# Seven block products for the input projection too, its results through DRAM, the mixers as a stage of two quarters

## The chip, the cores and the metric

One core of one Trainium2 chip runs the kernel, one launch for all of the work. The metric is device time in microseconds of that core, the median of several runs: 2829.16 us before the change (three runs, 2828.21 to 2831.07).

## What is computed

A decoder trunk of one layer on 2048 positions of width 1024, in float32. With h the RMS norm of x:

```
z = h @ w_in                       # 1024 x 5632: pool 512, conv value 512, conv gate 512, u 512, v 512, three gates of 1024
y_a = pool_mixer(z_pool)           # causal means over 2, 4, 8, 16 positions, less the input, then 128 x 256 products, scaled
y_b = silu(layernorm(dwconv31(val * sigmoid(gate)))) @ conv_pw
y_c = (gelu(u) * (causal 128 x 128 mix of layernorm(gelu(v)))) @ sgu_out
x = x + (sigmoid(g0 + b) * y_a + sigmoid(g1 + b) * y_b + sigmoid(g2 + b) * y_c) @ w_out
h = rmsnorm(x); z = h @ ffn_up     # 1024 x 5632, halves g and val
x = x + (silu(dwconv3(g)) * val) @ ffn_down
out = rmsnorm(x)
```

## The kernel before

The positions are cut into four quarters of 512, and two quarters make a half. Activations lie with channels on the 128 partitions and 512 positions along the free dimension; such a tile is a "half tile" of an arena of 67 (`Arena`, L105). To keep float32 accuracy each operand is split into a rounded part `hi` (a cast on ScalarE) and the rest `lo` (a subtraction on VectorE), in `split` (L263) for activations and in `ensure` (L180, lines 192 and 193) for weights, and each 128 x 128 x 512 product is three matmuls, `mm3` (L222, lines 225 to 227).

Weights come as chunks of 128 x 1024 in the order of the list `self.seq` through SyncE's queue, two ahead; up to four are prepared (`take`, `retire`). The order of TensorE, SyncE and GpSimd is the order of the program; VectorE and ScalarE are ordered by the planner, with `high_priority` for weights.

For each half, `build` (L1001) runs `mixers` (L516) and `w_out` (L730) for its first quarter, then for its second, then `ffn_up` (L836) for both, then `down` (L907) for each quarter. `mixers` makes the 44 column tiles of w_in one by one with `next_col` (L239; eight blocks deep, 24 matmuls) or, for u and v, with `rows` (L244), uses each where it lies, and drains the conv taps (`conv_taps`, L432, 31 VectorE instructions a tile) from a queue between products. Norms, pool means (L490), sgu (L453, L516) and the conv norm (L695) stand in this one stream. `w_out` stores the new x.

`ffn_up` treats two quarters as a 2 x 2 block product (two quarters by two halves of the 1024 channels, times the two halves of the channels by two column tiles) and makes it by seven block products of four blocks each (p1 to p7, `up_order`, L78) where eight would be plain. It needs sums and differences of the activations (`first_sums`, L770, `second_sums`, L790: the blocks a11, a12, s1 to s4, a22) and of the weights (`ready_part`, L158; four subtractions of GpSimd a column pair, L161). `down` fetches the stored activations for each of its two column halves and splits them (`queue_act`, L959). The first quarter's w_in starts on raw x and applies the norm behind the product for three conv pairs (`RAW_PAIRS`).

## Time and profile before

| | |
|---|---|
| median of three runs | 2829.16 us |
| the profiled execution, its span | 2830.14 us, 2828.4 us |
| TensorE busy, instructions | 2767.2 us (98%), 11938 |
| VectorE busy | 1978.9 us (70%) |
| ScalarE busy | 1167.3 us (41%) |
| GpSimd busy | 424.9 us (15%) |
| mean granted clock of TensorE | 0.988 |
| DMA | 361.13 MB, 128 GB/s |

The profile is of one execution, so sums are made against its own 2828.4 us and the 1.7 us around it. A busy TensorE is not yet one at its best, since matmuls overlap; their pitch is read from how many fall into a stretch. PE is TensorE, DVE VectorE, ACT ScalarE, POOL GpSimd, SP SyncE; L193 is a line of the kernel.

### The profile page before, as it was taken

The numbers are of one execution on the slowest core, as the hardware profiler recorded it, in microseconds if no ns is written. First come the engines' busy times: TensorE is split into PE (matmuls) and PEld (weight loads), VectorE is DVE, ScalarE is ACT, GpSimd is POOL, SyncE is SP. The second block draws the span as 40 slices with busy tenths as digits, with TensorE's granted clock in tenths as the row PEclk, the third lists the DMA queues.
The fourth block names the chain that finished last, engine by engine and source line by source line (L and its number), as shares of the span: only waits on it lengthen the run. The fifth ranks groups of instructions, "written<-read, shape, count | busy, mean of one in ns | idle before, by whom it ended". The sixth has DMA issues, their size and how long they took to land.

```text
span 2828.4 us, 32169 instructions
## 1 busy us (share of the span) xinstructions
PE 2767.2 (98%) x11938; PEld 2231.7 (79%) x11938; DVE 1978.9 (70%) x2980; ACT 1167.3 (41%) x1628; POOL 424.9 (15%) x326
## 2 busy tenths in 40 slices
PE   8999999999899999999999999999998999999998
PEld 7888888888688887787788888888886888877886
DVE  8995889658856565555689857896688556555565
ACT  4434324253544443445434343242534444434443
POOL 1000100000332332000200301000003332330020
PEclk9999999999899999999999999999998999999999
DMA  4224332333133233566432443323332233235564
GB/s 162 90 93 153 112 127 82 104 120 127 57 115 119 90 119 108 175 216 216 171 112 82 143 167 116 120 82 97 127 119 82 90 119 111 98 112 191 204 223 156
DMA packets 130013, 361.13 MB, mean 128 GB/s; under 512 B 14624, under 2 KB 16672, under 8 KB 129856
## 3 DMA queue, kind: packets, MB, share of 16 engines
q1 hardware_dynamic: 109296, 319.60, 33.8%
q10 hardware_dynamic: 18432, 32.51, 3.0%
q0 software_dynamic: 2128, 6.96, 0.6%
q8 instruction: 93, 1.52, 0.2%
q14 instruction: 64, 0.52, 0.1%
HBM read 318.65 MB, written 40.37 MB: 127 GB/s over the span
## 4 chain that ended last, share of the span: by engine, by line
PE 92%; DVE 3%; DMA 2%; POOL 1%; ACT 1%; issue 1%; SPq 0%; DVEq 0%; POOLq 0%; ACTq 0%
PE ps L226 30%; PE ps L227 30%; PE ps L225 30%; DVE h L268 1%; DMA both<-wts 1%; DVE wlo L193 1%; POOL tw L161 1%; DMA h<-act 1%; POOL h L355 0%; DMA h<-xT 0%; ACT whi L192 0%; PE ps L603 0%; ACT h L267 0%; PE ps L305 0%; PE ps L316 0%
## 5 line engine op out<-in xcount | busy, mean ns | idle before, releaser
L225 PE MATMUL ps<-h,whi 128*128 128x512 f32 x3648 | 1442.2, 395 | 27.1 <-ACT h L267 12.1
L226 PE MATMUL ps<-h,whi 128*128 128x512 f32 x3648 | 1442.1, 395 | 19.0 <-DVE h L268 18.5
L227 PE MATMUL ps<-h,wlo 128*128 128x512 f32 x3648 | 1439.0, 394 | 2.0 <-DVE wlo L193 1.9
L225 PEld LDWEIGHTS ps<-h,whi 128*128 128x128 f32 x3648 | 689.3, 189 | 192.1 <-ACT h L267 16.3
L226 PEld LDWEIGHTS ps<-h,whi 128*128 128x128 f32 x3648 | 689.1, 189 | 191.0 <-DVE h L268 33.8
L227 PEld LDWEIGHTS ps<-h,wlo 128*128 128x128 f32 x3648 | 689.9, 189 | 160.8 <-DVE wlo L193 4.2
L192 ACT CAST whi<-raw 128x1024 fp32r<-128x1024 f32 x376 | 394.2, 1050 | 891.0 <-PE ps L226 636.2
L193 DVE TENSOR_TENSOR wlo<-raw,whi 128x1024 fp32r<-128x1024 f32 x376 | 470.2, 1252 | 340.2 <-ACT whi L192 337.7
L444 DVE SCALAR_TENSOR_TENSOR h<-cbuf,params,h 128x512 f32<-128x512 f32 x480 | 340.6, 747 | 2.5
L193 DVE TENSOR_TENSOR wlo<-tw,whi 128x1024 fp32r<-128x1024 f32 x88 | 107.8, 1225 | 309.5 <-ACT whi L192 309.3
L161 POOL TENSOR_TENSOR tw<-both 128x512 f32<-128x512 f32 x88 | 122.9, 1396 | 1239.5 <-DMA both<-wts 1064.7
L268 DVE TENSOR_TENSOR h<-h,h 128x512 fp32r<-128x512 f32 x309 | 228.0, 764 | 68.0 <-ACT h L267 64.6
L267 ACT CAST h<-h 128x512 fp32r<-128x512 f32 x309 | 189.1, 619 | 183.9 <-DMA h<-act 75.3
L192 ACT CAST whi<-tw 128x1024 fp32r<-128x1024 f32 x88 | 92.4, 1050 | 212.7 <-POOL tw L161 119.5
L161 POOL TENSOR_TENSOR tw<-both,tw 128x512 f32<-128x512 f32 x88 | 156.5, 1778 | 3.4
L992 POOL TENSOR_TENSOR h<-h,h 128x512 f32<-128x512 f32 (+1 forms) x32 | 37.4, 1178 | 423.4 <-ACT h L982 422.9
L225 PE MATMUL ps<-whi,h 128*128 128x512 f32 x256 | 101.0, 395 | 0.0
L227 PE MATMUL ps<-whi,h 128*128 128x512 f32 x256 | 100.9, 394 | 0.0
L226 PE MATMUL ps<-wlo,h 128*128 128x512 f32 x256 | 100.7, 393 | 0.0
L355 POOL TENSOR_TENSOR h<-h,h 128x512 f32<-128x512 f32 x24 | 41.1, 1749 | 392.6 <-PE ps L227 375.4
L298 ACT ACTIVATE h<-h 128x512 f32<-128x512 f32 (+1 forms) x99 | 57.4, 609 | 39.1 <-DVE h L955 12.3
L299 DVE TENSOR_TENSOR h<-h,h 128x512 f32<-128x512 f32 (+1 forms) x82 | 58.9, 718 | 12.6 <-ACT h L298 9.5
(147 smaller groups left out, 1678.6 us busy)
## 6 DMA issues: line engine op xcount, KB each, us to landing
raw<-wts SPq DMA_DIRECT2D x376, 512.0 KB, 3.6
both<-wts SPq DMA_DIRECT2D x88, 512.0 KB, 4.5
h<-act SPq DMA_DIRECT2D x176, 256.0 KB, 4.1
act<-h ACTq DMA_DIRECT2D x88, 256.0 KB, 3.0
h<-xT SPq DMA_DIRECT2D x64, 256.0 KB, 5.4
x<-h ACTq DMA_DIRECT2D x32, 256.0 KB, 4.3
h<-x SPq DMA_DIRECT2D x32, 256.0 KB, 5.0
out<-h POOLq DMA_DIRECT2D x24, 256.0 KB, 2.7
```

The costliest lines, as they stand in the source:

```text
L161: sub = lambda o, a, b: self.nc.gpsimd.tensor_tensor(o, a, b, op=ALU.subtract)
L192: nc.scalar.copy(h, src)
L193: nc.vector.tensor_tensor(l, src, h.bitcast(F32), op=ALU.subtract)
L225: mm(out, l[0], r[0], start=start, stop=False)
L226: mm(out, l[0], r[1], start=False, stop=False)
L227: mm(out, l[1], r[0], start=False, stop=stop)
L267: self.nc.scalar.copy(hi, src)
L268: self.nc.vector.tensor_tensor(lo, src, hi.bitcast(F32), op=ALU.subtract)
L298: self.nc.scalar.activation(t, x, AF.Square)
L299: eng.tensor_tensor(s, s, t, op=ALU.add)
L355: nc.gpsimd.tensor_tensor(t, x[k], rstd, op=ALU.mult)
L444: nc.vector.scalar_tensor_tensor(acc, buf[:, k:k + T], w, acc, op0=ALU.mult, op1=ALU.add)
```

## The change

w_in is made for two quarters at once by the same seven block products (`w_in` on `strassen`, which `ffn_up` now shares): 22 pairs of column tiles, in an order given by `in_pairs`. Every result goes to DRAM after its activation function (`spill`, issued on SyncE's queue by `flush` two products later) and is fetched again where it is used. The order of the seven products is another one (`up_order`). The mixers become a stage for two quarters, which holds the sgu output, conv output and w_out products and reads gates and accumulators as streams.

What lay between the products becomes jobs, generators that are stepped once or twice per product (`tick`) as long as the arena has room: the rms factors of the second half (`factors_job`), the block sums of the next seven-product stage (`rows_job`), sgu mixing (`mix_job`, now with channels transposed and four matmuls of 128 columns a row tile), the pool (`pool_job`, window sums on GpSimd) and the conv norm (`conv_job`). The conv taps are drained one or two per product. The adds of squares and of the accumulators mostly move to GpSimd, which is now ordered by the planner.

The stages run: w_in of half 0; 15 of the 22 pairs of half 1; mixers of half 0; the other 7 pairs of half 1; ffn_up of half 0; down of quarter 0; mixers of half 1; down of quarter 1; ffn_up of half 1; down of quarters 2 and 3. `down` keeps its split activations for both column halves. The norm statistics always use the narrow form, and the first stage begins on normalized x (`head_rows`). The arena has 72 tiles.

```diff
-NHALF = 67
-RAW = 2
+NHALF = 72
+RAW = 3
...
+CUT = 15
...
+def in_pairs():
+
+    conv = [("conv", i, 512 + i * P, 1024 + i * P) for i in range(4)]
+    uv = [("uv", i, 1536 + i * P, 2048 + i * P) for i in range(4)]
+    pool = [("pool", i, 2 * i * P, (2 * i + 1) * P) for i in range(2)]
+    tiles = list(range(8)) + list(range(16, 24)) + list(range(8, 16))
+    gate = [("gate", (m, n), 2560 + m * P, 2560 + n * P) for m, n in zip(tiles[::2], tiles[1::2])]
+    rest = uv + pool + gate
+    return [p for i in range(4) for p in (conv[i], rest[2 * i], rest[2 * i + 1])] + rest[8:]
...
+def up_order(first=0, end=NPAIR):
+
+
+    out = [(p, first + i) for i in range(LAG) for p in ("p1", "p2")]
+    for i in range(first, end + 1):
+        n = i + LAG - 1 if i > first else end
+        out += [("p6", i), ("p4", i - 1), ("p5", i), ("p1", n), ("p7", i), ("p2", n), ("p3", i - 1)]
+    return [(p, i) for p, i in out if first <= i < end]
...
+        self.seq = w() + w(0, CUT) + mix + w(CUT, NPAIR) + up + down + mix + down + up + down * 2
...
+            raw = []
             for h in range(2):
-                self.nc.sync.dma_start(out=raw[:, h, :], in_=self.aps["wts"][i + h * NFF])
+                raw.append(self.wpool.tile([P, 1024], F32, name="raw", tag="raw", bufs=RAW))
+                self.nc.sync.dma_start(out=raw[h], in_=self.aps["wts"][i + h * NPAIR])
...
+    def room(self):
+
+        return len(self.halves.free) - (8 * (len(BLOCKS) - len(self.S)) if self.stage == "in" else 0)
...
+    def tick(self, n=1):
+
+        for _ in range(n):
+            for jobs in self.jobs:
+                if jobs and self.room() >= self.spare + jobs[0][1]:
+                    self.step(jobs)
...
+    def spill(self, dst, keys, t, flag=None):
+
+        self.fresh.append((dst, keys, t, flag))
+
+    def flush(self, n=1):
+
+        for _ in range(n):
+            for dst, keys, t, flag in self.due:
+                self.nc.sync.dma_start(out=dst, in_=t)
+                release(keys)
+                if flag:
+                    self.there[flag] = True
+            self.due, self.fresh = self.fresh, []
...
+    def block(self, st, name, k, t):
+
+        ks, p = self.split(t)
+        if st is None:
+            self.skeys.setdefault(name, []).extend(ks)
+            self.S.setdefault(name, []).append(p)
+            return
+        for d, key, s in zip(self.blocks[st][name][k], ks, p):
+            self.spill(d, [key], s.bitcast(F32), (st, name, k))
...
+    def factors_job(self, q):
+
+        yield 3
+        s = self.half()
+        for k in range(KD):
+            keys, (t,) = self.fetch([self.aps["xT"][q, k]])
+            self.add_square(s[1], t, self.nc.gpsimd, k == 0)
+            release(keys)
+            if k % 2:
+                yield 3
+        yield from self.rstd_job(self.rstx[q], s, ("rstx", q))
...
+        for k in range(H):
+            (k0, k2), (a0, b0) = nxt
+            yield 3
+            norm(a0, k, 0)
+            norm(b0, k, 1)
+            self.block(st, "a11", k, a0)
+            ks, s3 = self.half()
+            g.tensor_tensor(s3, a0, b0, op=ALU.subtract)
+            release([k0])
+            yield 3
+            (k3,), (b1,) = self.fetch([src[q0 + 1][k + H]])
+            self.block(st, "s3", k, s3)
+            yield
+            yield 2
+            norm(b1, k + H, 1)
+            self.block(st, "a22", k, b1)
+            g.tensor_tensor(b0, b0, b1, op=ALU.add)
+            g.tensor_tensor(b1, b1, s3, op=ALU.subtract)
+            release([ks])
...
+            for k in range(4):
+                c = slice(o * T + k * P, o * T + (k + 1) * P)
+                self.mm3(ps, (w[0][:, c], w[1][:, c]), self.S[moving[p]][k], start and k == 0, k == 3, not start)
...
+            if p == "p1":
+                g["s1"] = self.half()
+                cp(g["s1"][1], ps)
+            elif p == "p2":
+                k, t = g.pop("s1")
+                tt(t, t, ps, op=ALU.add)
+                sink(i, "11", t, k)
+            elif p == "p6":
+                g["u2"] = self.half()
+                cp(g["u2"][1], ps)
+            elif p == "p7":
+                k, t = self.half()
+                cp(t, ps)
+                tt(t, t, g["c"], op=ALU.add)
+                sink(i, "22", t, k)
+            elif p == "p4":
+                sink(i, "21", ps, None)
+            elif p == "p3":
+                k, t = g.pop("u2")
+                tt(t, t, ps, op=ALU.add)
+                sink(i, "12", t, k)
+                del st[i]
+            self.flush()
+            after(n - len(order))
+        self.flush(2)
...
+        for k in range(KC):
+            go = tap(k)
+            go.first = k == 0
+            go.flags = [("ci", n, i) for n in range(max(0, q - 1), q + 1)]
+            self.bg.append(go)
...
+    def w_in(self, q0, near, late=None, part=()):
...
+        def act(dst, t, key, func, flag, **kw):
+            k, s = (key, t) if key else self.half()
+            nc.scalar.activation(s, t, func, **kw)
+            self.spill(dst, [k], s, flag)
...
+            elif kind == "uv":
+                act((self.us, self.vs)[y][q][:, m * T:(m + 1) * T], t, key, AF.Gelu_apprx_tanh, ("uv"[y], q, m))
+            elif kind == "gate":
+                act(self.gates[q][m[y]], t, key, AF.Sigmoid, ("gate", q, m[y]),
+                    bias=self.par("bgate", m[y]))
...
+            nc.gpsimd.tensor_tensor(dst[:, lo:n], src[:, lo:n], src[:, lo - m:n - m], op=ALU.add)
...
+            pm = self.bank()
+            for h in range(4):
+                hs = slice(h * P, (h + 1) * P)
+                self.mm3(pm[:, hs], (x[0][:, hs], x[1][:, hs]), (sg[0][:, hs], sg[1][:, hs]), True, True)
+            for h in range(4):
+                hs = slice(h * P, (h + 1) * P)
+                nc.vector.scalar_tensor_tensor(t[:, hs], pm[:, hs], self.par("slg", h), bt[:, hs], op0=ALU.mult, op1=ALU.add)
+            nc.vector.tensor_tensor(t, t, ut, op=ALU.mult)
+            self.spill(heads(self.gt[q])[:, :, r * P:(r + 1) * P], [key], heads(t), ("gt", q, r))
+            release(ks + [ku])
...
+                for m in range(2):
+                    ps = self.col(w, [p for _, p in src[m]], off=(j % 2) * 512, nk=4)
+                    k, s = self.gstream()
+                    if n == 0:
+                        acc[j].append(self.astream())
+                    v.tensor_tensor(s, ps, s, op=ALU.mult)
+                    ka, a = acc[j][m]
+                    (v if n and j > 5 else g).tensor_tensor(a, a, s, op=ALU.add)
+                    release([k])
+                    if n:
+                        merged[m].append(self.split(a))
+                        release([ka])
+                    elif j > 4:
+                        for _ in range(1 + (j == 7)):
+                            cT[len(cT[0]) // 4].append(self.split_next(cstream))
+                    self.flush()
+                    during(n)
...
             for k in range(n):
-                self.queue_act(q, h, k + AHEAD)
+                if h == 0:
+                    self.queue_act(q, k + 2 * AHEAD)
                 if k % 2 == 0:
                     w = self.take()
-                ks, a = self.queued.pop((q, h, k))
-                step(w, k, range(F4), slice(0, T), a)
...
-        key, t = self.half()
-        self.nc.sync.dma_start(out=t, in_=self.acts[q][k])
-        self.queued[q, h, k] = self.split(t)
+        (key,), (t,) = self.fetch([self.acts[q][k]])
+        self.queued[q, k] = self.split(t)
...
+        self.add(self.setup_sgu(), self.factors_job(2), self.factors_job(3))
+        self.add(self.rows_job("w1", 2, xT, "nmix", self.rstx[2:], [("rstx", 2), ("rstx", 3)]))
+        self.add(self.open_mix())
+        for q in (0, 1):
+            self.add(self.mix_job(q, range(NR)))
+        self.add(self.close_mix())
+        for q in (0, 1):
+            self.add(self.pool_job(q, range(4)), self.conv_job(q))
+
+
+        def near(n):
+            self.spare = 7 if n > -20 else 3
+            if n + TOTAL > 8:
+                self.tick()
+            self.drain(2 if self.there["w1"] else 1)
+            self.next_blocks("w1", n)
+
+        self.w_in(0, near, late)
...
+        self.w_in(2, near, None, (0, CUT))
...
+        self.add(self.open_mix(), side=1)
+        for r in range(NR):
+            for q in (2, 3):
+                self.add(self.mix_job(q, [r]), self.pool_job(q, [r]), side=r)
...
+        def later(j):
+            self.tick(2)
+            self.drain(1)
+            if j > 4:
+                self.fetch_block("w1", BLOCKS[j - 5])
+
+        self.mixers(0, during, later)
...
+        self.add(self.rows_job("f0", 0, self.x1, "nffn", self.rst[:2], [("rst", 0), ("rst", 1)]))
...
+        self.w_in(2, near, None, (CUT, NPAIR))
...
+        def near(n):
+            m = n + TOTAL
+            self.fetch_rest("f0", m, (0, 1))
+            self.drain(1 + (m % 4 == 0))
+            if -4 <= n:
+                self.queue_act(0, 2 * n + 8)
+                self.queue_act(0, 2 * n + 9)
+
+        self.ffn_up(0, near)
...
+        x = self.down(0, True, each, done(0, nc.gpsimd))
...
+        self.mixers(2, during, later)
+        self.add(self.rows_job("f1", 2, self.x1, "nffn", self.rst[2:], [("rst", 2), ("rst", 3)]))
...
+        def each(h, k):
+            self.tick(2)
+            if h and k in (10, 13, 16, 19):
+                if k == 10:
+                    self.need("f1")
+                self.fetch_block("f1", BLOCKS[(k - 10) // 3])
+
+        x = self.down(1, True, each, done(1, nc.gpsimd))
```

## Rows read from the trace of the kernel before

**Rows 1.** The page: busy time of each engine, and the chain by engine.

```profile
PE 2767.2 (98%) x11938; PEld 2231.7 (79%) x11938; DVE 1978.9 (70%) x2980; ACT 1167.3 (41%) x1628; POOL 424.9 (15%) x326
...
PE 92%; DVE 3%; DMA 2%; POOL 1%; ACT 1%; issue 1%; SPq 0%; DVEq 0%; POOLq 0%; ACTq 0%
```

**Rows 2.** Table by stretches, FFN: engines' busy us (instructions), clock, DMA share, GB/s.

```profile
750.00:1100.00 350.00, 350.00 (x1514) 284.12 (x1514) 212.22 (x348) 148.59 (x200) 112.49 (x72) 1.00 0.30 107
```

**Rows 3.** Table by stretches, TensorE alone, where matmuls are missing.

```profile
0.00:20.00 20.00, 12.99 (x47) 1.00 0.68 239
...
720.00:760.00 40.00, 29.58 (x91) 0.79 0.09 32
...
1120.00:1180.00 60.00, 56.02 (x233) 0.97 0.52 175
...
1280.00:1400.00 120.00, 109.54 (x449) 0.94 0.54 187
...
2120.00:2160.00 40.00, 29.56 (x91) 0.79 0.11 40
...
2520.00:2580.00 60.00, 54.95 (x224) 0.97 0.44 146
```

**Rows 4.** Instructions in order of time near the end, TensorE: start us, us, what.

```profile
2802.40 0.28 PE L226 MATMUL ps<-h,whi 128*128 128x256 f32 x1
...
2804.64 0.28 PE L227 MATMUL ps<-h,wlo 128*128 128x256 f32 x1
```

**Rows 5.** The chain of waits in order of time: start us, us, what.

```profile
125.72 1.75 PE ps L603 x16
...
705.12 0.79 PE ps L316 x8
```

**Rows 6.** Instructions in order of time, the start.

```profile
6.92 0.80 PE L225 MATMUL ps<-h,whi 128*128 128x512 f32 x1 [6.92 <-ACT h L1011]
...
7.92 4.00 ACT L1011 ACTIVATE h<-h,params 128x512 fp32r<-128x512 f32 x6 [0.44 <-DMA h<-xT]
...
12.86 1.04 ACT L192 CAST whi<-raw 128x1024 fp32r<-128x1024 f32 x1
...
22.24 1.05 PE L316 MATMUL ps<-ones,h 128*128 128x1 f32 x8 [0.29 <-DVE h L1018]
...
26.86 0.75 DVE L351 SCALAR_TENSOR_TENSOR h<-h,params,ps 128x512 f32<-128x512 f32 x1 [0.74 <-PE ps L324]
```

**Rows 7.** The page: costliest groups, VectorE and ScalarE: busy us, mean ns.

```profile
L444 DVE SCALAR_TENSOR_TENSOR h<-cbuf,params,h 128x512 f32<-128x512 f32 x480 | 340.6, 747 | 2.5
...
L193 DVE TENSOR_TENSOR wlo<-tw,whi 128x1024 fp32r<-128x1024 f32 x88 | 107.8, 1225 | 309.5 <-ACT whi L192 309.3
...
L267 ACT CAST h<-h 128x512 fp32r<-128x512 f32 x309 | 189.1, 619 | 183.9 <-DMA h<-act 75.3
```

**Rows 8.** Groups by shape, VectorE: busy us, mean ns, idle before.

```profile
L881 DVE TENSOR_TENSOR h<-h,ps 128x512 f32<-128x512 f32 x44 | 30.2, 687 | 0.0
```

**Rows 9.** Table by stretches, the first quarter's mixers, all engines.

```profile
50.00:343.00 293.00, 293.00 (x1279) 238.01 (x1278) 246.01 (x382) 114.90 (x164) 14.92 (x10) 1.00 0.33 108
```

**Rows 10.** Instructions in order of time, VectorE and GpSimd in the FFN stage.

```profile
803.16 1.29 POOL L161 TENSOR_TENSOR tw<-both 128x512 f32<-128x512 f32 x1
...
804.32 1.23 DVE L193 TENSOR_TENSOR wlo<-tw,whi 128x1024 fp32r<-128x1024 f32 x1 [2.46 <-ACT whi L192]
...
804.41 2.29 POOL L161 TENSOR_TENSOR tw<-both,tw 128x512 f32<-128x512 f32 x1
...
805.49 0.69 DVE L890 TENSOR_TENSOR h<-h,ps 128x512 f32<-128x512 f32 x1
```

**Rows 11.** Instructions in order of time, VectorE and GpSimd at the next quarter's norm.

```profile
1374.88 3.45 DVE L268 TENSOR_TENSOR h<-h,h 128x512 fp32r<-128x512 f32 x2
...
1370.98 10.22 POOL L355 TENSOR_TENSOR h<-h,h 128x512 f32<-128x512 f32 x6 [17.20 <-issue]
```

**Rows 12.** Instructions in order of time, issues on SyncE's queue.

```profile
1287.44 4.72 SPq L371 DMA_DIRECT2D h<-xT  x8
```

More of the change, by code (lines that the diff above doesn't have):

```diff
@@ L102, in up_parts @@
+def up_parts(*pairs):
+    out = []
+    for p, i in up_order(*pairs):
+        if (OF[p][0], i) not in out:
+            out.append((OF[p][0], i))
     return out
@@ new lines, in rstd_all @@
+        for r in range(nr):
+            nc.tensor.matmul(ps[:, r:r + 1], s[:, r * P:(r + 1) * P], self.ones, start=True, stop=True)
+        v = self.small.tile([P, NR], F32, name="ms", tag="ms", bufs=4)[:, 0:nr]
+        with self.tc.high_priority(QUICK):
+            nc.vector.tensor_scalar(v, ps[:, 0:nr], 1.0 / n, eps, op0=ALU.mult, op1=ALU.add)
+            y = self.rsqrt(v, nr)
+        yield
+        out = self.bank()[:, 0:nr * P]
+        for r in range(nr):
+            nc.tensor.transpose(out[:, r * P:(r + 1) * P], y[:, r:r + 1].to_broadcast([P, P]), self.ident)
@@ L698, in conv_norm, with conv_job @@
+    def conv_job(self, q):
+        nc = self.nc
+        while not all(self.there["cv", q, i] for i in range(4)):
+            yield
+        yield 4
+        ck, c = self.fetch(self.cv[q])
+        yield
+        yield
+        yield 3
         ks, s = self.half()
-        c = [t for _, t in conv]
         nc.vector.tensor_tensor(s, c[0], c[1], op=ALU.add)
@@ L910, in down @@
+    def down(self, q, last, each, done, tail=None):
         nc = self.nc
@@ L932, in down @@
                 if k == n - 8:
[L933 removed]
+                    new = self.fetch(self.x1[q][F4 * h:F4 * (h + 1)])
                     keys += new[0]
                     x += new[1]
[L936 to L937 removed]
+                self.flush()
                 each(h, k)
@@ new lines, in build, with end @@
+        self.ffn_up(2, near)
+        x = self.down(2, False, lambda h, k: None, done(2, nc.vector))
+        self.add(self.later(4, self.final(2, x, got[2])))
+        fb = []
+        def end(j, ts, x):
+            s = got[3]
+            self.add_square(s[1][:, ts], x[1][j][:, ts], nc.vector, False)
+            if ts.start and j == KD // 2 + 1:
+                next(fb[0])
+            if j == KD - 1:
+                if ts.start:
+                    next(fb[0])
+                fb.append(self.final(3, x, s, ts, 1 + (ts.start > 0)))
```

1248 lines of the change are left out of this document (602 added, 646 removed).

## The prediction

> **What bounds the kernel now.** I read the page's busy times first. TensorE is busy for 2767.2 us of 2828.4, and the chain of waits puts 92% of the span on its three matmul lines, VectorE 3%, DMA 2% [rows 1]. So time is the number of matmuls times their pitch, plus the gaps. The table by stretches gives the pitch: 1514 matmuls in 350 us without a gap is 350 / 1513.5 = 0.2312 us [rows 2] (each stretch also counts the matmuls that straddle its edges, about 1.5). The same view shows the gaps, each as the matmuls that fit less those that ran [rows 3]: the first 20 us (41 missing, 9.5 us), the entry to each seven-product FFN stage at 720 and 2120 (83 missing, 19.3 us each, at a mean granted clock of 0.79, so partly at the lower level of 1.2 GHz), 1280 to 1400 (71, 16.5 us: the next quarter's norm inside the second down product), 1120 to 1180 (28, 6.5) and 2520 to 2580 (37, 8.6). With the tail that is nearly all that is not dense matmul. VectorE is not the bound, but in the mixers stretch it is busy 246 of 293 us while TensorE has no gap [rows 9]; the reader should keep that 84%.
>
> **The change part by part.**
>
> Matmuls removed. w_in was 44 column tiles x 8 x 3 = 1056 matmuls a quarter, 4224 in all. By seven products it is 22 pairs x 7 x 4 x 3 = 1848 for two quarters, 3696 in all. 528 fewer x 0.2312 = -122.1 us. ffn_up (3696), down, the pool, sgu, conv and output products keep their counts.
>
> Small matmuls. Sgu mixing goes from 48 of 512 columns to 192 of 128. No row shows a split matmul of 128 columns. The nearest are 256 columns at 0.118 us (twenty starts from 2802.40 to 2804.64) and float32 transposes of 128 at 1.75 / 16 = 0.109 [rows 4, 5]. Bounds: half of 0.118, or a full 0.2312. I take 0.118, since both nearest rows lie there: 192 x 0.118 - 48 x 0.2312 = +11.6 us (0 to +33). The rms and layer norm sums go to the narrow form: 72 more one-column matmuls at 0.79 / 8 = 0.099 [rows 5], 36 more transposes at 0.109, 16 fewer wide ones: +7.1 + 3.9 - 3.7 = +7.3.
>
> Stage entries removed. The FFN's sums are now made by a background job, written to DRAM and fetched before the stage begins, so both entries of 19.3 us go: -38.6. The 16.5 us of 1280 to 1400 go too, since no quarter norm sits in a down product any more: -16.5. What comes late next at these places is priced below under entries.
>
> The start. Today the first matmul runs at 6.92 on raw x, with the norm applied behind. After the change it needs the normalized x. The squares are summed by 22.24 now, behind eight raw splits on ScalarE (six in 4.00 us, so 5.3) and two weight casts of 1.04; without these 7.4 us, about 14.8. From sum to factor took 22.24 to 26.86, 4.6 us; then a norm, a cast and a subtraction, 0.75 + 0.62 + 0.69 [rows 6 to 8]. First matmul near 21.5, some 14 us later. Behind it the seven products start as the FFN does today, the second quarter's sums being made while the first ones run, which cost 19.3. Together +33 (+14 if the second part hides, +50 if VectorE, which also prepares weights there, takes half as much again).
>
> VectorE's work. Call w_in of the first half and the first 15 pairs of the second the dense stretch: 37 pairs, 37 x 84 x 0.2312 = 719 us of matmul, with the 40 of the start about 759. In program order VectorE gets there, by the durations of [rows 7, 8] (1.23 for a wide weight subtraction, 0.747 for a tap, 0.69 for any 512 columns): weights 37 x (3 x 1.23 + 0.69) = 162; three combinations a pair at 0.69, 77; conv taps, one to two a product, about 347 x 0.747 = 259; the head's sums 42; the second half's sums 31; eight sgu row tiles at 5.1, 41; pool 26; conv norms 25; conv products and splits 16. Sum 680, 90% of the stretch. Elsewhere VectorE loses work: each activation is split once instead of twice (88 x 0.69 = -61), and rsqrt is done on four columns, not 512. I cost these at nothing: it has slack there.
>
> GpSimd's work is new. The stretch gets 4 weight subtractions a pair (148), 20 window sums of the pool, 14 squares of the factors, 14 of the head and 16 of the sums: 212 operations. The rows show that the two engines hold each other up. Alone a subtraction takes 1.29 us; the one at 804.41 took 2.29 while VectorE's weight subtraction ran from 804.32 undisturbed, and VectorE's combination out of PSUM at 805.49 ran undisturbed beside it [rows 10]. Where both queues are full it is VectorE that waits: two subtractions took 3.45 us for 1.38, while GpSimd did six in 10.22 [rows 11]. So one GpSimd operation takes (3.45 - 1.38) / 2 = 1.04 us of what VectorE needs when both its inputs lie in SBUF. Of VectorE's 680 us about 142 read PSUM or are tiny; 538 + 212 x 1.04 = 758 against 759, so with perfect interleaving nothing is lost; with every operation in VectorE's way 680 + 220 = 900, 141 lost. I take +40: weights are prepared two parts ahead, so GpSimd can often be the one that waits, as at 804.41, and that is the commoner row.
>
> ScalarE gets 3 x 44 copies and loses 58 casts of weights and 88 of activations; it is at 41% now [rows 1] and I cost it at nothing, covered as long as VectorE is the later of the two.
>
> Transfers. All stores and fetches go through SyncE's queue, some 1700 issues by my count of the code, twice today's. A row of eight issues took 4.72 us, 0.59 each [rows 12], so 1700 are about a third of the span. Stores are issued two products after their result, behind which weight loads wait. In the first half of the mixers stage a product of 2.8 us needs a gate, an accumulator, half a conv tile, a quarter weight and about 1.6 issues of jobs: 4.4 issues (2.6 us) and about 1.1 MB. The first 20 us moved 239 GB/s [rows 3], by which 1.1 MB take 4.6 us, so 16 products could lose 29 us; at its busy share of 0.68 full engines would give 351 GB/s and 3.1 us, 5 us lost. The seven new entries of stages, where up to 8 MB of sums are fetched within some ten products, stand beside today's 6.5 and 8.6. Together I take +20 (0 to +80), near the lower end because most is fetched ahead.
>
> Sum: 2828.4 - 122.1 + 11.6 + 7.3 - 38.6 - 16.5 + 33 + 40 + 20 = 2763.1. The profiled execution took 2830.14, 1.7 around its span; the median of the runs is 1.0 below it. 2764 us.
>
> **A rule against the change.** The GPSIMD Engine Reference of the Trainium skill (Specifications) says that GpSimd's way into SBUF is shared with VectorE, and that VectorE's instructions with two SBUF inputs, or in its two-port mode, contend for it. The rows above agree for two inputs, with 1.04 us each time; taken to its end the rule gives the first rival below, which is priced by those rows alone.
>
> **The rivals.**
>
> Slower: VectorE and GpSimd together become the bound of the dense stretch. Place: those 37 pairs. Price: the full 141 us in place of 40, 2764 + 101 = 2865. It decides from 105 us lost there, since 2764 - 40 + 105 is today's time. For it: the two-for-one rows of full queues, and taps and jobs come by count of products, so VectorE can't put them off. Against it: 84% with no gap today, and a late VectorE is shed again in the stages behind.
>
> Faster: TensorE stays fed everywhere, as in today's 350 us of FFN, where GpSimd is busy a third of the time [rows 2]: neither the 40 nor the 20 are paid, 2704.
>
> Transfers: the mixers and the entries pay their full 80 instead of 20, 2824 at the worst and about 2805 in the middle. For it: all goes through one queue in order. Against: the streams run three to four tiles ahead.
>
> No gain: the saved matmuls are spent on gaps that come from several of these at once, at about 2829.
>
> **Numbers.** Forecast 0.50 (own range 2735 to 2795), fed 0.22 (2690 to 2735), transfers 0.10, no gain 0.04, VectorE with GpSimd 0.14. A difference of 0.2%, 5.7 us, is about what a measurement can tell: faster 0.82, same 0.04, slower 0.14. Range 2695 to 2850: it leaves out the far part of the slower case and a little of the fed one, and takes the bounds of the start, the entries and the small matmuls in.
>
> **What would show it.** TensorE's instructions fall by 528 and rise by 144 + 92 (the new small ones less the old): about 11,646 in place of 11,938 [rows 1]. The first matmul at 21 to 22 us. No fall of the granted clock at the entry of either FFN stage. In the dense stretch, up to about 800 us, VectorE at 90% or more, GpSimd at 30% or more, and TensorE's waits on lines of weight preparation or of the combinations, some 40 us in all; if they are under 10 the fed case holds, if over 100 the slower one. VectorE's subtractions with two SBUF inputs above 0.69 us there. The prediction is wrong in its main term if the pitch in the w_in stage is not 0.231, and wrong in its working if the gaps lie in the mixers stage behind DMA.

## The result and the profile after

The changed kernel takes 3049.65 us (median of 4 runs, 3047.29 to 3056.03); the kernel before, run beside it, 2828.68. The ratio is 1.0783, with a 95% interval of 1.0764 to 1.0802: slower by 221 us, where 2764 was forecast and the range ended at 2850.

The page of the kernel after: busy times, TensorE's share and its granted clock in 40 slices, and the chain of waits by engine.

```profile
PE 2750.1 (90%) x11646; PEld 2199.7 (72%) x11646; DVE 2075.9 (68%) x2880; ACT 1143.1 (38%) x1613; POOL 886.3 (29%) x660
...
PE   4898889899983889978899999999998899999998
...
PEclk8999999999995889988899999999998999999999
...
PE 43%; DVE 7%; DMA 3%; issue 2%; ACT 1%; POOL 1%; SPq 0%; DVEq 0%; ACTq 0%; POOLq 0%
```

Against [rows 1] TensorE has 292 instructions less and GpSimd twice as many. The shares of the chain add up to 57% only, since this view follows it back from the end to 1328 us and no further; so its 43% can't be set beside the 92% before. The page of e7_ffntaps, which differs in one line of the program (see below), has the whole chain:

```profile
PE 58%; DVE 21%; DMA 8%; issue 6%; POOL 4%; ACT 2%; SPq 1%; DVEq 0%; POOLq 0%; ACTq 0%
```

The kernel after by stretches; columns as in [rows 2] (length, then TensorE, weight loads, VectorE, ScalarE, GpSimd, clock, DMA share, GB/s).

```profile
20.00:100.00 80.00, 49.71 (x172) 35.89 (x172) 57.46 (x78) 34.23 (x51) 33.44 (x22) 0.80 0.21 68
150.00:550.00 400.00, 358.15 (x1495) 284.34 (x1496) 315.39 (x425) 161.06 (x233) 139.93 (x93) 0.95 0.58 190
...
900.00:1000.00 100.00, 39.67 (x108) 26.18 (x109) 51.78 (x86) 20.88 (x32) 20.32 (x18) 0.59 0.54 183
...
1250.00:1400.00 150.00, 123.24 (x476) 94.40 (x475) 106.56 (x126) 57.33 (x86) 58.38 (x39) 0.89 0.82 291
1425.00:1465.00 40.00, 34.68 (x133) 26.41 (x133) 15.26 (x25) 14.59 (x19) 6.46 (x6) 0.90 1.05 396
...
1450.00:1600.00 150.00, 134.99 (x549) 106.83 (x548) 133.38 (x183) 53.24 (x74) 44.69 (x30) 0.93 0.43 146
1700.00:1800.00 100.00, 100.00 (x433) 81.01 (x432) 71.44 (x97) 41.85 (x56) 27.34 (x20) 1.00 0.37 124
...
2320.00:2350.00 30.00, 24.37 (x85) 18.85 (x84) 15.42 (x27) 10.89 (x16) 5.77 (x4) 0.79 1.04 389
```

433 matmuls fit into 100 us, as 1700 to 1800 shows. In 900 to 1000 there are 108, at a clock of 0.59: TensorE was held up so often that it also ran at 1.2 GHz. And 150 to 550 lacks 235 of 1730 matmuls (54 us) with VectorE busy for 79%, not 90%.

TensorE's waits in the kernel after: line waited for, us in all, times, longest.

```profile
PE ps L285 <- ACT h L308: 74.2, 16, 9.8
PE ps L287 <- DVE wlo L207: 52.5, 27, 6.1
PE ps L285 <- ACT whi L206: 34.4, 14, 10.4
PE ps L363 <- DVE rs_y L331: 24.6, 7, 9.1
PE ps L355 <- DVE h L473: 22.0, 2, 13.7
...
PE ps L285 <- DMA h<-w1s: 2.6, 1, 2.6
```

Casts of activations and weights on ScalarE (L308, L206) and the weights' subtractions on VectorE (L207) lead. Transfers end 3 us of TensorE's waits directly; what they cost through operands that come late is not in that number.

For the comparisons below I use one count. A stage runs from its first product's matmul to that of the next stage; its loss is its length less its matmuls at 0.2312 us each (0.118 for 256 columns, 0.1 for narrower ones), from their starts in the trace. A is the first half's w_in, B the first 15 pairs of the second half's, C the first half's mixers, D the other 7 pairs, E the first half's FFN products; F, G and H are down product, mixers and down product; I is the second half's FFN products. The last two down products lose under 9 us in every run and are left out.

| loss, us | A | B | C | D | E | F+G+H | I |
|---|---|---|---|---|---|---|---|
| after | 113.6 | 108.8 | 41.5 | 55.2 | 34.7 | 4.2 | 30.0 |
| e1_room | 119.1 | 59.5 | 31.1 | 56.2 | 34.7 | 2.6 | 28.0 |
| e2_poolorder | 112.2 | 109.7 | 59.0 | 62.1 | 38.8 | 3.3 | 19.8 |
| e3_taps | 72.5 | 72.6 | 31.1 | 40.6 | 11.5 | 4.2 | 26.6 |
| e4_nosub | 62.6 | 85.6 | 43.3 | 45.3 | 12.2 | 4.7 | 15.0 |
| e5_three | 49.2 | 1.6 | 16.9 | 27.4 | 12.0 | 3.6 | 15.5 |
| e6_order | 111.5 | 93.2 | 43.6 | 67.5 | 39.3 | 4.5 | 34.2 |
| e7_ffntaps | 115.1 | 109.6 | 41.3 | 58.3 | 21.2 | 3.9 | 28.5 |
| e8_idlesub | 109.6 | 108.3 | 43.4 | 56.9 | 27.3 | 2.3 | 18.1 |
| e9_spread | 112.5 | 30.0 | 44.1 | 59.6 | 16.1 | 22.8 | 27.8 |
| e10_prio | 113.9 | 61.2 | 30.0 | 56.9 | 34.6 | 4.9 | 26.1 |
| e11_cache | 137.2 | 22.5 | 30.8 | 42.8 | 37.8 | 6.7 | 17.4 |
| e12_all | 132.8 | 1.2 | 41.0 | 42.4 | 25.6 | 27.2 | 17.1 |
| e13_head | 119.1 | 58.4 | 30.8 | 56.8 | 35.0 | 3.6 | 27.7 |
| e14_parts | 137.5 | 10.9 | 29.7 | 46.3 | 26.9 | 3.6 | 15.9 |

The second half's stages behind E are fed, but for the entry of I. All the rest is lost in the first 1900 us. By the same count, the first ten products of E lose 20.2 us and those of I 29.8 (all of I's loss) in the kernel after.

### The profile page after: what moved, and what is told of

Same layout as the page of the kernel before. It is cut to its first block, busy times and chain, and to the rows that moved or that the text cites. A ratio compares the mean times of both kernels' runs of the same rounds, so it can differ in the third digit from the quotient of the medians.

```text
span 3045.6 us, 33650 instructions
## 1 busy us (share of the span) xinstructions
PE 2750.1 (90%) x11646; PEld 2199.7 (72%) x11646; DVE 2075.9 (68%) x2880; ACT 1143.1 (38%) x1613; POOL 886.3 (29%) x660
## 3 DMA queue, kind: packets, MB, share of 16 engines
q10 hardware_dynamic: 1152, 1.05, 0.1%
## 4 chain that ended last, share of the span: by engine, by line
PE 43%; DVE 7%; DMA 3%; issue 2%; ACT 1%; POOL 1%; SPq 0%; DVEq 0%; ACTq 0%; POOLq 0%
PE ps L287 14%; PE ps L285 14%; PE ps L286 14%; DVE h L688 2%; DVE wlo L207 2%; DMA h<-f0s 1%; DMA cbuf<-ci 0%; DMA raw<-wts 0%; DMA f0s<-h 0%; DMA h<-f0a 0%; DVE h L309 0%; DVE h L1050 0%; DVE h L1051 0%; DVE h L1076 0%; POOL tw L176 0%
## 5 line engine op out<-in xcount | busy, mean ns | idle before, releaser
L285 PE MATMUL ps<-h,whi 128*128 128x512 f32 x3696 | 1486.0, 402 | 89.0 <-ACT whi L206 34.4
L286 PE MATMUL ps<-h,whi 128*128 128x512 f32 x3696 | 1476.0, 399 | 15.1 <-DVE h L309 14.5
L176 POOL TENSOR_TENSOR tw<-raw 128x512 f32<-128x512 f32 x176 | 253.6, 1460 | 1114.7 <-DMA raw<-wts 1009.5
L207 DVE TENSOR_TENSOR wlo<-raw,whi 128x1024 fp32r<-128x1024 f32 (+1 forms) x296 | 385.6, 1304 | 254.4 <-ACT whi L206 252.4
L688 DVE SCALAR_TENSOR_TENSOR h<-cbuf,params,h 128x512 f32<-128x512 f32 x480 | 429.1, 894 | 8.2
L206 ACT CAST whi<-raw 128x1024 fp32r<-128x1024 f32 (+1 forms) x296 | 272.3, 920 | 391.3 <-PE ps L286 350.2
L308 ACT CAST h<-h 128x512 fp32r<-128x512 f32 x300 | 183.1, 619 | 389.9 <-POOL h L994 80.8
L206 ACT CAST whi<-tw 128x1024 fp32r<-128x1024 f32 x176 | 184.2, 1047 | 271.4 <-POOL tw L176 161.6
L207 DVE TENSOR_TENSOR wlo<-tw,whi 128x1024 fp32r<-128x1024 f32 x176 | 225.1, 1281 | 86.3 <-ACT whi L206 83.2
L176 POOL TENSOR_TENSOR tw<-raw,tw 128x512 f32<-128x512 f32 x176 | 264.0, 1500 | 6.8
L340 POOL TENSOR_TENSOR h<-h,h 128x512 f32<-128x512 f32 x62 | 94.6, 1526 | 320.3 <-ACT h L339 297.3
L654 DVE TENSOR_TENSOR h<-h,ps 128x512 f32<-128x512 f32 x88 | 60.2, 684 | 144.3 <-ACT h L653 142.5
L994 POOL TENSOR_TENSOR h<-h,h 128x512 f32<-128x512 f32 x56 | 84.3, 1514 | 123.3 <-DVE h L992 105.6
L646 DVE TENSOR_TENSOR h<-h,ps 128x512 f32<-128x512 f32 x88 | 60.2, 684 | 85.4 <-PE ps L287 82.9
L1166 POOL TENSOR_TENSOR h<-h,h 128x512 f32<-128x512 f32 (+1 forms) x32 | 38.1, 1217 | 267.8 <-ACT h L1156 267.7
```

What stands on the lines that cost most here:

```text
L176: sub = lambda o, a, b: self.nc.gpsimd.tensor_tensor(o, a, b, op=ALU.subtract)
L206: nc.scalar.copy(h, src)
L207: nc.vector.tensor_tensor(l, src, h.bitcast(F32), op=ALU.subtract)
L285: mm(out, l[0], r[0], start=start, stop=False)
L286: mm(out, l[0], r[1], start=False, stop=False)
L308: self.nc.scalar.copy(hi, src)
```

## The experiments

Two theories stood against each other: that TensorE waits because jobs' matmuls stand in its written order before their operands can be ready, and that VectorE and GpSimd are too loaded to feed it. The "port theory" in the expectations is a form of the second: GpSimd's accesses to SBUF hold VectorE up.

**e1_room.**

```
-            self.spare = 7 if n > -20 else 3
+            self.spare = 3
...
-            self.spare = 7 if m < 45 else 3
+            self.spare = 3
```

> The jobs' threshold of free tiles is 3 in both w_in stages of the first half, where the changed kernel asks for 7 over the last 20 products of the first and the first 45 of the second. Nothing is left out of the computation. Written-order theory: the jobs then advance at nearly every product, few of them are left to be forced at the end of the second stage, and 900 to 1000 us, where 108 matmuls ran of 432, fills up: about 75 us less, 2975 (2955 to 3000), with the other stages within 15 us of now. Load theory (VectorE and GpSimd together are the bound there): the same work only comes earlier, into stretches that are as loaded, and the time stays within 25 us of 3050.

2990.45 us, ratio 1.0563 [1.0545, 1.0581]: 59 us less than the changed kernel. By the code's own count of free tiles, followed through the order in which it writes the program, the jobs were refused at nearly every product from 137 of A to 47 of B, for want of 7 free tiles, and at product 102 of B `need`, which steps jobs until a result that is now due exists, forced 74 steps of jobs between two products, the pool groups of both quarters among them. In TensorE's order their matmuls then stood directly behind the sums that feed them. The kernel after there (start, us, what, idle before and its end):

```profile
908.54 0.80 PE L285 MATMUL ps<-h,h 128*128 128x512 f32 x1 [8.80 <-ACT h L308]
920.84 0.79 PE L285 MATMUL ps<-h,h 128*128 128x512 f32 x1 [9.08 <-ACT h L308]
930.36 0.80 PE L285 MATMUL ps<-h,h 128*128 128x512 f32 x1 [6.28 <-ACT h L308]
941.64 1.52 PE L346 MATMUL ps<-h,wide_ones 128*128 128x512 f32 x2 [8.05 <-ACT h L308]
...
962.57 0.79 PE L285 MATMUL ps<-h,h 128*128 128x512 f32 x1 [9.84 <-ACT h L308]
```

With a threshold of 3, `need` forces no step in B, and these waits are gone (B 108.8 to 59.5, C 41.5 to 31.1). The written-order theory holds for this part, and the other stages show that it isn't the whole.

**e2_poolorder.**

```
-engines={mybir.EngineType.PE, mybir.EngineType.SP}
+engines={mybir.EngineType.PE, mybir.EngineType.SP, mybir.EngineType.Pool}
```

> GpSimd's instructions stand in the order in which the code issues them, as in the kernel before, in place of the planner's. Nothing is left out. If the planner's order keeps window sums and sums of squares behind weight subtractions whose transfers are late, the written order gives back 10 to 40 us of the job matmuls' waits (3010 to 3040). If on the contrary it is what brings weights in time, waits on weights grow by 20 to 60 us (3070 to 3110). The written-order theory for TensorE alone expects under 15 us either way, since the forced steps at the end of the second stage stay.

3062.5, ratio 1.0824 [1.0807, 1.0840]: 13 slower, as the third of the expectations has it, though not evenly: C loses 17.5 us more and I 10.2 less. The change had also given GpSimd's order to the planner, which I hadn't priced. In sum that is not where the time went; at the entry of I, GpSimd's order does matter (see below).

**e3_taps and e4_nosub.**

```
-        for k in range(KC):
+        for k in (0, KC - 1):
```

> 29 of the 31 taps of the depthwise convolution are left out (464 VectorE instructions at 0.89 us, 415 us, nearly all of them before 1600 us). Load theory: of the 222 us lost in the two dense w_in stages over two thirds go, with the third and fourth stages some 250 us in all: 2800 to 2890. Written-order theory: the hole at 900 to 1000 us stays (75 us) and only the small waits on casts and weights shrink, 40 to 90 us less: 2960 to 3010.

```
             self.both = raw
+        return self.both[what == "t3"]
```

> The 352 weight subtractions on GpSimd are left out: the products take raw quarters of the weights in their place, with the same transfers and casts. Port theory (GpSimd's subtractions hold VectorE up): taps go back from 0.89 to about 0.75 us, the waits on weights (87 us over the run) and the small waits go, 100 to 150 us less: 2900 to 2950. Written-order theory: the hole at 900 to 1000 us stays, the waits on weights shrink by half, 30 to 60 us less: 2990 to 3020.

2917.13 (1.0309 [1.0293, 1.0324]) and 2926.86 (1.0347 [1.0332, 1.0363]): 133 and 123 us less. e3_taps lies between the two theories' numbers. e4_nosub lies inside the port theory's, though its taps come down to 785 ns and not 750, and 33 us of waits on weights stay. They take 41 and 51 us from A, and 23 each from E; neither clears the hole of B.

**e8_idlesub** keeps GpSimd's subtractions and lets nobody read them.

```
             sub(t[:, H:], b21, self.t2)
-        return t
+        return self.both[what == "t3"]
```

> GpSimd still does its 352 weight subtractions, into the same tiles, but nothing reads them: the products take the raw quarters, as in e4_nosub (so the sums of weights are left out of the products). Port theory: the cost is that GpSimd's accesses hold VectorE up, so it is all still paid: within 25 us of 3050. Chain theory: the cost is that a weight goes through transfer, GpSimd, ScalarE and VectorE one after the other, so the time is near that of e4_nosub: 2915 to 2950.

3032.84, ratio 1.0726 [1.0708, 1.0744]. Of the 123 us that the subtractions cost, 106 are still paid when no product waits for them; taking them out of the weights' chain alone brings 17. By the table I gains 11.9 from that and E 7.4, while A to D change by 4 or less. The trace says how the 106 are paid. Page and costliest groups (busy us, mean ns), first without the subtractions (e4_nosub, where line numbers are one higher), then with unread ones (e8_idlesub), then the kernel after:

```profile
PE 2714.2 (93%) x11646; PEld 2182.0 (75%) x11646; DVE 1871.8 (64%) x2880; ACT 1149.5 (39%) x1613; POOL 372.0 (13%) x308
...
L208 DVE TENSOR_TENSOR wlo<-raw,whi 128x512 fp32r<-128x512 f32 (+1 forms) x472 | 556.5, 1181 | 375.3 <-ACT whi L207 373.7 <-DMA h<-f1s 0.2 <-DMA x<-h 0.2
...
L689 DVE SCALAR_TENSOR_TENSOR h<-cbuf,params,h 128x512 f32<-128x512 f32 x480 | 377.0, 785 | 8.0
...
L1054 DVE SCALAR_TENSOR_TENSOR h<-fhalo,params,h 128x1 f32<-128x1 f32 x88 | 20.1, 229 | 1.4
...
L655 DVE TENSOR_TENSOR h<-h,ps 128x512 f32<-128x512 f32 x88 | 60.3, 685 | 162.1 <-ACT h L654 156.6 <-DMA h<-xT 5.5
```

```profile
PE 2740.1 (91%) x11646; PEld 2192.2 (72%) x11646; DVE 2087.4 (69%) x2880; ACT 1142.4 (38%) x1613; POOL 898.5 (30%) x660
...
L207 DVE TENSOR_TENSOR wlo<-raw,whi 128x512 fp32r<-128x512 f32 (+1 forms) x472 | 628.3, 1333 | 352.3 <-ACT whi L206 347.5 <-DMA cbuf<-ci 3.7 <-DMA raw<-wts 0.3
...
L688 DVE SCALAR_TENSOR_TENSOR h<-cbuf,params,h 128x512 f32<-128x512 f32 x480 | 427.2, 890 | 8.0
...
L1053 DVE SCALAR_TENSOR_TENSOR h<-fhalo,params,h 128x1 f32<-128x1 f32 x88 | 53.9, 613 | 1.3
...
L654 DVE TENSOR_TENSOR h<-h,ps 128x512 f32<-128x512 f32 x88 | 60.2, 684 | 72.9 <-ACT h L653 72.8
```

```profile
L688 DVE SCALAR_TENSOR_TENSOR h<-cbuf,params,h 128x512 f32<-128x512 f32 x480 | 429.1, 894 | 8.2
...
L654 DVE TENSOR_TENSOR h<-h,ps 128x512 f32<-128x512 f32 x88 | 60.2, 684 | 144.3 <-ACT h L653 142.5 <-DMA us<-h 1.7
```

The same 2880 VectorE instructions take 215.6 us longer with 352 unread GpSimd subtractions beside them, 0.61 us for each (204.1 us longer in the kernel after, where they are read). The taps, both tensors in SBUF, go from 785 to 890 ns (747 in [rows 7]), the weights' subtractions from 1181 to 1333, and a halo instruction of a single column, which reads two tiles of SBUF, from 229 to 613; the additions that read PSUM stay at 684. The GPSIMD Engine Reference of the Trainium skill (Specifications) names VectorE instructions with two SBUF inputs, beside those in a two-port mode, as the ones that contend with GpSimd for SBUF. These rows agree: the instructions with two SBUF inputs grow, those with one input in PSUM don't.

One rival is to be looked at: an unread subtraction still reads the raw weight tiles, so it could hold them and delay the next load. SyncE's waits before the loads of L161 speak against it (us, times, longest; e8_idlesub, e4_nosub, then the kernel after): with unread subtractions the loads wait for VectorE as long as without any, and GpSimd, which holds them for 237 us in the kernel after, ends 1.4 us of them in e8_idlesub.

```profile
SPq L161 <- DVE wlo L207: 585.5, 144, 13.6
```

```profile
SPq L161 <- DVE wlo L208: 585.4, 144, 13.5
```

```profile
SPq L161 <- POOL tw L176: 237.0, 61, 6.5
```

**e5_three** is e1_room, e3_taps and e4_nosub together.

> The three edits e1_room, e3_taps and e4_nosub together (so 29 of 31 taps and GpSimd's weight subtractions are left out). If their gains are of separate causes they add: 59 + 132 + 123 us less, 2736. If taps and subtractions cost through one thing, the two engines' common load, the second of them brings little once the first is gone: 59 + 133 + some 20 to 50, so 2810 to 2840. The rest, above 2690 us, is what start, stage entries and jobs cost with nothing in VectorE's way.

2783.54, ratio 0.9842 [0.9827, 0.9856]: 266 less, between the two expectations (sum 315). So the causes overlap by 48 us; that fewer taps leave less for GpSimd to hold up would explain it, but no run shows that. B is fed to within 2 us. It leaves out work and is no version to use; it shows that the plan of seven products would take 1.6% off the kernel before, were these three absent.

**e6_order** puts the products in the order before.

```
+    for i in range(first, end):
+        n = i + LAG
+        if n < end:
+            out += [("p6", i), ("p5", i), ("p7", i), ("p1", n), ("p4", i), ("p2", n), ("p3", i)]
...
```

> The seven products stand in the order of the kernel before (p6 p5 p7 p1 p4 p2 p3 of a pair, three pairs ahead) in all four stages; nothing is left out. Order theory: t3 and x1 are held for fewer products, weights are prepared earlier, the two FFN stages lose under 15 us each in place of 35 and 30, and the w_in stages 20 to 50 in all less: 2960 to 3000. Load theory: VectorE has the same work, and p7's copy and addition come closer to p4: within 25 us of 3050.

3053.35, ratio 1.0795 [1.0779, 1.0811], no difference. Waits on weights fall from 87 to 38 us, and waits on the copies of p6 and p7 rise from 32 to 109, since these products now lie closer (TensorE's waits, e6_order; L289 and L291 are the first and third matmul of `mm3`, L654 and L657 the copies):

```profile
PE ps L289 <- ACT h L654: 61.3, 18, 13.9
PE ps L289 <- ACT h L657: 48.0, 27, 7.5
PE ps L289 <- ACT whi L210: 25.2, 7, 10.3
PE ps L291 <- DVE wlo L211: 12.7, 10, 3.6
```

Which line TensorE is seen to wait on follows from the order; how long, it does not.

**e7_ffntaps.**

```
-            self.drain(1 + (m % 4 == 0))
+            self.drain(m % 2)
```

> In the first FFN stage the convolution's taps come at one every second product, where the changed kernel gives five in four; the rest of them runs in the down product behind it. Nothing is left out. Load theory: that stage loses 10 to 18 us in place of 35, and nothing comes back later, since the down product leaves VectorE idle: 3025 to 3033. If the stage's loss comes from the new order of products or from the shared ring of raw weights, it stays at 30 or more: 3045 to 3055.

3038.28, ratio 1.0742 [1.0726, 1.0758]: 11 less, E 34.7 to 21.2. It missed both bands, by 5 us the load theory's, which had E at 10 to 18. The same 90 taps run in the stage in either kernel, and VectorE has nearly the same work (about 370 us), but evenly, instead of mostly in the first half: its load over a part of the stage counts, and not only the sum.

**e10_prio** puts the copies and additions out of PSUM first in the planner's order.

```
+                with self.tc.high_priority(QUICK):
+                    cp(t, ps)
+                    tt(t, t, g["c"], op=ALU.add)
```

> e1_room with the copies and additions that empty PSUM put ahead of other work in the planner's order on ScalarE and VectorE (a priority of 30). Nothing is left out. If TensorE waits because these stand behind taps and casts in the engines' queues, the waits on copies of p6 and p7 (some 35 us) go with the low clock behind them: 2940 to 2970. If the two engines are simply short of time, weights come later by as much: within 15 us of 2990.

2987.29, ratio 1.0561 [1.0543, 1.0578]; e1_room has 2990.45. TensorE's waits on the copies of p6 and p7 stay, 40 us in place of 41. Their place in the queue isn't the cause.

**e9_spread, e11_cache, e12_all** leave nothing out.

```
-            self.drain(2 if self.there["w1"] else 1)
+            self.drain(1)
...
-            self.drain(1 + m % 2)
+            self.drain(1 + (m % 4 == 0))
...
-            self.drain(1 + (m % 4 == 0))
+            self.drain(m % 2)
```

> e1_room with the taps spread: one a product in the first w_in stage (two before, from its middle on), five in four in the second (three in two), one every second product in the first FFN stage; the rest runs in the down product behind it. Nothing is left out. Load theory: some 84 taps leave the dense stages, A and B lose 25 to 40 us less and the FFN stage 11 to 15 less, nothing comes back in the down product: 2945 (2930 to 2960) against 2990 of e1_room. If the waits are only a matter of where chains stand in TensorE's order, 2980 or more.

```
+        elif what in ("c2", "c3"):
+            raw = self.wpool.tile([P, 1024], F32, name="raw", tag="raw", bufs=RAW)
+            self.nc.sync.dma_start(out=raw, in_=self.made["t" + what[1], i])
...
+        self.made[what, i] = self.dram.tile([P, 1024], F32, name=f"made{what}_{i}", tag=f"made{what}_{i}", bufs=1)
+        self.nc.gpsimd.dma_start(out=self.made[what, i], in_=t)
```

> e1_room where the sums of weights that GpSimd makes in the first w_in and the first FFN stage are stored to DRAM (by GpSimd's own queue, 512 KB each) and read back by the second half's stages, so that half of the 352 subtractions go and nothing is left out of the computation. Port theory: the second w_in (both parts) and the second FFN stage gain what they gained in e4_nosub, 23 + 10 + 15 us, and the stores cost the first ones 0 to 15: 2950 (2935 to 2970). If the stores crowd the transfers, 2990 or more.

> The edits of e9_spread and e11_cache together with e1_room. Nothing is left out. By the load theory with the port both gains are had, less some overlap: 2905 (2885 to 2935). It stays above the kernel before (2828), since the first w_in stage keeps its subtractions.

2975.36 (1.0521 [1.0505, 1.0537]), 2949.54 (1.0430 [1.0412, 1.0448]) and 2945.04 (1.0413 [1.0398, 1.0429]). e9_spread and e12_all missed: the taps put off come due in F and G, which lose 20 us more, and in C. e11_cache is as expected in sum, but not by stages: B gains 37 us where 23 were expected, and the stores cost A 18 where 0 to 15 were, so two errors cancel. Stage B allows a comparison, 280 us in the middle of it in e1_room, e11_cache and e12_all:

```profile
610.00:890.00 280.00, 249.94 (x1041) 199.26 (x1039) 231.57 (x289) 107.34 (x148) 101.16 (x72) 0.95 0.51 165
```

```profile
610.00:890.00 280.00, 268.47 (x1163) 217.29 (x1162) 232.90 (x336) 123.50 (x168) 27.80 (x24) 0.98 0.64 209
```

```profile
610.00:890.00 280.00, 279.80 (x1222) 227.10 (x1221) 215.79 (x310) 131.55 (x182) 27.91 (x24) 1.00 0.65 211
```

VectorE is busy for 83% in the first two. With 72 GpSimd instructions it gets 289 done (0.80 us each), with 24 of them 336 (0.69): part of the busy time of the first is being held up, and looks like work. TensorE runs 122 matmuls more; the weights' shorter chain has a share in that, which this pair of runs doesn't separate. With fewer taps as well, TensorE has no gap.

**e13_head and e14_parts.**

```
-        f = sums(1)
-        next(f)
+        with self.tc.high_priority(2 * PREP):
+            f = sums(1)
+            next(f)
```

> e1_room where the squares and sums of the second quarter's norm stand ahead of all else in the planner's order on ScalarE, VectorE and GpSimd, in place of behind the first t2 weight's cast. Nothing is left out. In-order theory of the start: VectorE stood idle from 33.5 to 37.6 us behind that weight, which waited for GpSimd and a transfer; with the sums ahead TensorE's wait at 42.5 (8.3 us) goes, all of the start comes 5 to 9 us earlier and the low clock is shorter: 2975 to 2985 against 2990. If the start is set by the chain behind it (norm, sums, splits of the second quarter), the wait only moves: 2988 to 2993.

2989.41, ratio 1.0567 [1.0552, 1.0581]: nothing, as the second theory had it. The wait of 8.3 us at 42.5 goes, but by product 14 both have lost 43.4 and 43.5 us. From 20 to 50 us, e1_room and then e13_head:

```profile
20.00:30.00 10.00, 6.47 (x16) 4.05 (x16) 8.74 (x12) 6.01 (x10) 1.37 (x1) 1.00 0.17 57
30.00:40.00 10.00, 3.09 (x6) 1.68 (x6) 5.97 (x9) 3.20 (x5) 6.68 (x4) 0.54 0.39 125
40.00:50.00 10.00, 7.47 (x26) 6.32 (x27) 5.79 (x14) 1.04 (x1) 4.03 (x3) 0.61 0.09 38
```

```profile
20.00:30.00 10.00, 5.33 (x10) 2.42 (x9) 9.63 (x13) 4.69 (x7) 1.76 (x1) 1.00 0.12 33
30.00:40.00 10.00, 6.96 (x21) 4.60 (x19) 5.94 (x12) 3.90 (x6) 6.74 (x4) 0.99 0.38 133
40.00:50.00 10.00, 7.77 (x17) 5.30 (x18) 6.14 (x11) 1.66 (x2) 5.05 (x4) 0.50 0.13 45
```

Without the wait 15 matmuls more run between 30 and 40 us, but 6 fewer before it and 9 fewer behind it, with short waits on splits and at a clock of 0.50, which is 1.2 GHz: by 50 us both kernels have run as many. From 60 to 70 us VectorE is busy throughout in both (10.00 us of 10, 6 matmuls), mostly with the second quarter's norm, sums and splits, on which TensorE waits there.

e14_parts is e1_room, e11_cache and e13_head with the taps of B and E slowed.

> e1_room, e11_cache and e13_head together, with taps at five in four products in the second w_in stage and one in two in the first FFN stage (the rate of the first w_in stage as in the changed kernel, so that few taps are left for the down product). Nothing is left out. If the gains add without being paid back later, 2949 of e11_cache less 15 to 20 (second w_in stage), 10 to 12 (FFN stage) and 5 to 9 (start): 2910 (2900 to 2925). If what is taken from one stage is paid in the next, as from e11_cache to e12_all, 2935 or more.

2927.74, ratio 1.0355 [1.0341, 1.0369]. It missed by 3 us of its band: B and E gain 11.6 and 10.9 on e11_cache and little is paid behind. It is the fastest of the versions that compute everything, 122 us below the changed kernel and 100 above the one before; none is as fast as the kernel before.

## Why the prediction was wrong

**Right.** TensorE has 11,646 instructions to the number, at 0.231 us where it is fed. The first matmul of a product came at 22.7 (21 to 22 forecast). Twelve sgu matmuls of 128 columns take 1.17 us from the first start to the last where their operands are ready, 0.107 apart, for the 0.118 taken. Transfers end only 3 us of TensorE's waits directly.

**The sizes.** My sum left 141 us for all that isn't matmul (2764, less 1.7 around the span and 2621 for the matmuls that ran, at the prices of the count above); the kernel has 425 (22.7 to the first matmul, 394.5 in the stages, 7.5 behind). Term by term:

| term | forecast | measured |
|---|---|---|
| start, to product 14 | 42.5 (9.5 of before + 33) | 65.5 (22.7 + 42.8) |
| VectorE and GpSimd in the dense stretch (A, B) | 40 | 130 (A behind product 14: 70.8; B without the forced jobs: 59.5) |
| jobs forced at once | 0 | 60 (49 in B, 10 in C) |
| C, D and both FFN stages | 20 (transfers, with the new entries) | 151 (C without the forced jobs 31.1, D 55.2, E 34.7, I 30.0) |
| the rest | 39 | 18 |

**The step that failed** in the dense stretch is the one of GpSimd: "I take +40: weights are prepared two parts ahead, so GpSimd can often be the one that waits". There 130 us were lost; without taps and subtractions and with the lower threshold (e5_three) it is 14 (A behind product 14: 12.3; B: 1.6). VectorE is the one that pays, 0.6 us for each of 352 subtractions, and TensorE pays half of that (e8_idlesub against e4_nosub: 215.6 us of VectorE, 106 of the total). I had measured a dearer price, 1.04 us for each of two subtractions [rows 11], and then let the milder row [rows 10] decide. The slower rival had the place right, and nearly the price (141; 130 measured), at a chance of 0.14; its 2865 fell short by the terms that stand below it in the table.

**Its reach.** The largest part of the miss lies behind A and B: 131 of 284 us. I priced VectorE in the dense stretch alone and everything behind at nothing but the transfers' 20. But the weights' subtractions and the taps go on through D and E, and the subtractions through I: without the taps E loses 11.5, without the subtractions E and I lose 12.2 and 15.0, in place of 34.7 and 30.0.

**The entries.** That "both entries of 19.3 us go: -38.6" failed as well: the first ten products of E and I lose 20.2 and 29.8 us, and the clock that was not to fall there is 0.90 from 1425 to 1465 and 0.79 from 2320 to 2350. I had the sums of the activations made ahead, but not what the entries then ask of GpSimd and of the transfers. In stage I the weights' subtractions stand in GpSimd's queue behind the first half's last multiplications and their stores (L1166, L1167, of `final`), and TensorE waits for their cast:

```profile
2356.14 2.49 POOL L1166 TENSOR_TENSOR h<-h,h 128x512 f32<-128x512 f32 x2
...
2359.16 3.42 POOL L176 TENSOR_TENSOR tw<-raw 128x512 f32<-128x512 f32 x2
...
2363.83 1.04 ACT L206 CAST whi<-tw 128x1024 fp32r<-128x1024 f32 x1 [7.64 <-POOL tw L176]
...
2364.93 0.80 PE L285 MATMUL ps<-h,whi 128*128 128x512 f32 x1 [10.39 <-ACT whi L206]
```

So stage I loses 18.1 when no product waits for the subtractions (e8_idlesub) and 19.8 with GpSimd in written order (e2_poolorder): here most of their price is the chain, and little the holding up of VectorE. At the entry of E the DMA engines are busy throughout (1.05 and 396 GB/s from 1425 to 1465, by the table of stretches), and the chain of waits goes through transfers one after another from 1414 to 1467 us. e5_three still loses 10.5 and 14.8 us in the first ten products of E and I. How much of that is the transfers', as the rival of that name had it, no run shows, since none made them fewer there.

**Its sign.** I looked for saturation, VectorE at 90%. It was at 79% between 150 and 550 us, and TensorE still lacked 54 us. In [rows 9] VectorE is busy for 84% and TensorE has no gap, with GpSimd at 5%. The busy share alone doesn't tell: it counts held time, and each product needs its operands from several engines in order. Why TensorE starves at 79% instead of 90% no run resolves; that less work on either engine lessens it, e3_taps and e4_nosub show (A behind product 14: 70.8 to 26.5 and 26.3), and in B it ends (e12_all).

**What was missing.** That jobs advance only while 3 or 7 tiles are free, and that `need` makes up for it at one point in TensorE's order, stood in the code. I had read it as bookkeeping; it cost 60 us in B and C (59 of the whole, e1_room).

**The start** cost 23 us more than forecast, 6 over my bound. It isn't one wait: e13_head removed the one that looked largest and won nothing.

Open: even in e5_three C loses 17 us, D 27, E 12, I 16 and A's first 14 products 37, so some 72 of the 151 us behind B have no shown cause; a deeper ring of prepared weights wasn't tried.

## What to carry to other kernels

Before trading TensorE's matmuls for sums on other engines, price the sums: a pair here saves 12 matmuls (2.8 us) and its four GpSimd subtractions alone take 2.4 us of VectorE. Count GpSimd's elementwise work on SBUF as VectorE time in every stage, not only where VectorE looks full, and at the entry of a stage look at what stands before it in GpSimd's queue. For work that is interleaved by a condition, count when the program is written how often the condition refuses, and what is forced where.

## What the runs showed of the hardware

A GpSimd subtraction of 512 columns costs VectorE 0.61 us on average over the run (e8_idlesub against e4_nosub), through instructions with two SBUF inputs (785 to 890 ns for a tap, 967 in e1_room's dense stretch), and nothing for additions that read PSUM (684 in all). An instruction of a single column pays as well: 229 to 613 ns for the halo of the FFN's convolution, 88 times. The tap's durations there, e1_room and then e11_cache, 610 to 890 us:

```profile
L688 DVE SCALAR_TENSOR_TENSOR h<-cbuf,params,h 128x512 f32<-128x512 f32 x118 | 114.1, 967 | 2.1
```

```profile
L695 DVE SCALAR_TENSOR_TENSOR h<-cbuf,params,h 128x512 f32<-128x512 f32 x143 | 115.1, 805 | 2.7
```

A wait of 8.3 us taken away from TensorE at the start brought nothing by 50 us; its clock was 0.50 between 40 and 50 us, where the kernel with the wait had 0.61 (e13_head).
